# A hybrid decoder layer on one core: the memory loaded transposed with its 1/rms applied at the keys and values, and the final norm in an order written out by hand

## The chip, the cores and the metric

The kernel runs on one core of a Trainium2 chip. The time is device time in microseconds (us) of one execution; the number compared is the median over runs. The engines are TensorE (PE, matrix products; PEld is its loading of weights), VectorE (DVE), ScalarE (ACT), GpSimd (POOL) and SyncE (SP), which here only issues loads. Every engine takes its own instructions in order.

## The reference

One layer on 512 tokens of 1024 channels, with 256 memory tokens, everything in fp32. A mixer with three gated branches, a cross-attention to the memory and a squared-ReLU MLP each add to x; a last norm gives the output. What the change touches:

```python
def rmsnorm(x, g):
    y = x * rsqrt(mean(x * x, axis=-1) + EPS)
    return y * g
...
mem_n = rmsnorm(mem, norm_mem_g)
k, v = split(mem_n @ w_kv, 2)                     # 256 memory tokens, 4 heads x 256
sc = einsum('bshd,bmhd->bhsm', q, k) * 256 ** -0.5
o = einsum('bhsm,bmhd->bshd', softmax(sc), v)
...
x = x + squared_relu_mlp(rmsnorm(x, norm_mlp_g), w_up, w_down)
return rmsnorm(x, final_g)
```

Since 1/rms is one number per token, it commutes with the product: (r * mem * g) @ w = r * ((mem * g) @ w).

## The kernel before

**Products.** Each fp32 operand is split into a high part in the matrix engine's fp32r type and a low part, the rest; a product is three (high x high, high x low, low x high: `mm3`, lines 361 to 363). Weights arrive in chunks of 512 KB on SP's queue (line 304) and are split on the chip: ScalarE casts (line 112), VectorE subtracts (line 113). `split` (lines 350, 351) does this for activations, `split_scaled` (355, 356) with a factor, a number or one value per partition.

**Seven products for eight.** The projections w_o, w_xo and w_down go through `items_w`: a block of 1024 channels is done as seven block products, P1 to P7, of 24 matrix instructions each (line 493). Sums of weights are formed by VectorE (line 131, `plus`) or by a DMA that adds (line 236); results are added to x from the PSUM banks by `add` (lines 128 and 131). For w_o (class `Early`) the order is P1, P2 and P5 in turns, then P6, P3, P7, P4; for w_down (class `Wide`) P1 and P5 in turns, then P6, P3, P2, P7, P4. P7 and P4 finish tokens 256 to 511 (t = 2, 3); P4 goes row by row, so t = 2 is done before t = 3. The hook `after(p)` puts work behind a product.

**Norms.** `norm_begin` sums the squares of half a row block on ScalarE (line 562); `norm_end` does the other half, forms 1/rms (VectorE line 566, GpSimd's power line 556) and multiplies by it and by the gain, which lies broadcast over all partitions (line 584). `norm_T` transposes the result on TensorE (line 593, eight 128 x 128 blocks per 128 tokens, into two PSUM banks of the tag "at") and splits it.

**The memory.** `mem_begin` loads on GpSimd's queue the broadcast gain (512 KB) and the memory's 256 rows (two tiles m_sb of 512 KB). Behind P5 of w_o `mem_norm` norms both tiles; behind P6 and P3 `norm_T` transposes one each into mT (channels on partitions). Then `kv_proj` makes the keys, eight blocks of 24 products with mT moving (256 columns), and the values (mT stationary); `xk_done` and `xv_done` split what comes out. Between the key blocks stand the transposes of the layer's own norm for t = 2, 3. GpSimd's queue is in the written order in this part (`reload_x` enters `manual_schedule` for it).

**The final norm.** Behind P3 of the last block of w_down `norm_begin` sums the finished right halves of t = 0, 1, behind P2 `final` ends them; behind P7 and P4 the same is done for t = 2, 3. `final` is, per t: square sum of the left half, 1/rms, then two products on VectorE (line 1307, left and right 512 columns), each followed by its store, the left on SP's queue, the right on ScalarE's (line 1309).

**Order.** The program is a list of items (`plan`); weights are fetched and split two steps ahead (`pump`, `AHEAD`). The order in which each engine gets its instructions is made before the run by a planner that simulates the kernel with modelled times and goes by the program's order where more than one instruction could go (`schedule_with_timeline_sim`). Inside a `manual_schedule` the named engines keep the program's order. Two of the four "at" banks hold one accumulator from P1 through P6, P7 and P4, two the other from P5 through P3 (`part`, bank names p1 and p3), so that P3's adds free the first two for transposes and P4's adds the others. The large tiles share 30 slots (`unit`), short-lived ones nine (`scr`).

Of the kernel before, what the change touches and what calls it, by code (L numbers as in the profile page):

```python
# [10 lines left out]
F32 = mybir.dt.float32  # L11
F32R = mybir.dt.float32r
AF = mybir.ActivationFunctionType
ALU = mybir.AluOpType
# [24 lines left out]
def trunk_kernel(ctx: ExitStack, tc: tile.TileContext, x, mem, par, rot, dqd, kdec, g_mix, g_xa, g_mem, g_mlp,  # L39
# [50 lines left out]
    gmx = const.tile([P, KT], F32, name="gmx")  # L90

# [381 lines left out]
    def items_w(src, c, pairs, after=lambda p: None, kind=Wide):  # L473
# [4 lines left out]
        def part(p, js, n):  # L478
            bank = dict(P2="p2", P5="p3", P3="p3").get(p, "p1")

            def fn(ws):
# [21 lines left out]
                for i, j in [(i, j) for i in range(2) for j in js] if rows else [(i, j) for j in js for i in range(2)]:  # L503
                    mm(i, j)
                    if j == 1:
                        add(i)
            item(fn, (kind, src, c, n, n + len(js)))
# [45 lines left out]
    def rstd_of(ms, n):  # L553

        r = small.tile([P, n], F32, name="rstd")
        pool.tensor_tensor(out=r, in0=ms, in1=half[:, :n], op=ALU.pow)
        return r
# [516 lines left out]

    def mem_begin():
        S["g_mem"] = load_g(g_mem, pool)
        S["m_sb"] = [unit("m_sb", (P, D), F32) for _ in range(2)]
        for t in range(2):
            pool.dma_start(out=S["m_sb"][t], in_=mem[t * P:(t + 1) * P, :])

    def mem_norm():
        S["mT"] = Split("mT", KT, MEM)
        for t in range(2):
            norm_begin(("m", t), S["m_sb"][t])
            norm_end(("m", t), S["m_sb"][t], S["g_mem"])

    def mem_beside(p):
        if p == "P5":
            item(mem_norm)
        if p in ("P6", "P3"):  # L1090
            t = int(p == "P3")
            item(lambda: norm_T(("m", t), S["mT"], t))
# [24 lines left out]
    def proj_norm(src, name, g, beside, after, first=lambda its: None, kind=Early):  # L1117
# [20 lines left out]
        its = capture(lambda: items_w(src, 0, lambda k: S[name, k // 2].w[k % 2], ends, kind))  # L1138
# [13 lines left out]
    def xk_done(d):  # L1152
        def fn(ps):
            hi, lo = S["kT"](d)
            split(hi, lo, ps[:, :MEM])
        return fn

    def xv_done(c):
        def fn(t, ps):
            hi, lo = S["xv"](t)  # L1160
            cs = slice(c * 512, (c + 1) * 512)
            split(hi[:, cs], lo[:, cs], ps)
        return fn
# [137 lines left out]
    def final(t):  # L1301
        y, ss = S["xn", t], S["ss", t]
        sumsq(S["x"][t], 0, ss, 1, y)
        r = norm_rstd(ss)
        for c, eng in ((0, nc.sync), (1, act)):
            cs = slice(c * 512, (c + 1) * 512)
            dve.scalar_tensor_tensor(out=y[:, cs], in0=S["x"][t][:, cs], scalar=r, in1=S["g"][:, cs],
                                     op0=ALU.mult, op1=ALU.mult)
            eng.dma_start(out=out[t * P:(t + 1) * P, cs], in_=y[:, cs])

    def last(p):
        if p == "P3":
            def begin():
                S["g"] = load_g(g_fin, pool)
                for t in (0, 1):
                    norm_begin(t, S["x"][t], 1)
            item(begin)
        if p == "P2":
            item(lambda: [final(t) for t in (0, 1)])
        if p == "P7":  # L1320
            item(lambda: [norm_begin(t, S["x"][t], 1) for t in (2, 3)])
        if p == "P4":
            item(lambda: [final(t) for t in (2, 3)])

    def down(r):
        items_w(w_down, 8 * r, lambda k: S["u", 2 * r + k // 2].w[k % 2], last if r == NP // 4 - 1 else lambda p: None)
# [66 lines left out]

def _pack_b(w):
# [5 lines left out]
def _lay_out(i):  # L1400
# [10 lines left out]
        "mem": a["mem"][0],  # L1411
# [4 lines left out]
        "g_mix": col(a["norm_mix_g"][0]), "g_xa": a["norm_xa_g"][0], "g_mem": a["norm_mem_g"][0],  # L1416
# [39 lines left out]
```

## Time and profile before

| | us |
|---|---|
| median of 3 runs (1014.11 to 1016.59) | 1015.11 |
| profiled execution, its own time | 1016.54 |
| its span, first to last instruction | 1014.8 |
| TensorE busy | 994.1 |
| VectorE busy | 715.6 |
| ScalarE busy | 526.6 |
| GpSimd busy | 73.4 |

Mean granted TensorE clock: 0.994 of full speed. In the groups a line reads: line of the program, engine, operation, output <- inputs, shape, count, then busy time and mean duration in ns, and behind the bar the idle time ahead of these instructions with what ended it. In a timeline a line begins with start and length in us, and brackets hold a wait and its releaser. Times are from the span's start. A matrix instruction's length includes its way through the pipeline; what it costs in a row of them is the distance between starts.

### The profile page before, as it was taken

Reading aid. Unit: us, or ns where it says so; the run is one execution under the profiler, and the core shown is the slowest. Engines: PE = TensorE matmul, PEld = TensorE weight load, DVE = VectorE, ACT = ScalarE, POOL = GpSimd, SP = SyncE. Lnnn points to the kernel's source line nnn. Section 1 sums busy time; section 2 is a strip of 40 time slices with the busy share of each in tenths; the row PEclk is TensorE's granted clock in tenths of the full one; section 3 lists DMA queues with packets and bytes.
Section 4 is the critical chain, followed back from the end, with each engine's and each line's share of the span. In section 5 each row is a group of like instructions: output and inputs, shape, how many; then the busy total and the mean of one; then the engine's idle time right before and its main releaser. Section 6 shows DMA issues by size and latency. Waiting matters only on the chain.

```text
span 1014.8 us, 13137 instructions
## 1 busy us (share of the span) xinstructions
PE 994.1 (98%) x4958; PEld 841.1 (83%) x4958; DVE 715.6 (71%) x1064; ACT 526.6 (52%) x908; POOL 73.4 (7%) x135
## 2 busy tenths in 40 slices
PE   8999999999999999999989999999999999999996
PEld 6788888878888889988788888879888888888885
DVE  5757787777463787779785466875785785695785
ACT  6556666766433344444654346655544543553543
POOL 1001111223110000001100001110000000000001
PEclk9999999999999999999989999999999999999998
DMA  9332223222122212334555225642044125115212
GB/s 361 129 132 83 83 84 117 80 74 84 63 103 70 77 59 90 122 137 165 169 173 186 84 84 125 165 147 85 20 142 148 43 95 175 63 47 186 80 42 84
DMA packets 32176, 113.08 MB, mean 111 GB/s; under 512 B 3952, under 2 KB 3952, under 8 KB 32112
## 3 DMA queue, kind: packets, MB, share of 16 engines
q1 hardware_dynamic: 28224, 99.65, 28.1%
q0 software_dynamic: 2880, 10.49, 4.4%
q10 hardware_dynamic: 1008, 2.10, 0.6%
q8 instruction: 39, 0.64, 0.2%
q14 instruction: 25, 0.20, 0.1%
HBM read 110.13 MB, written 2.10 MB: 111 GB/s over the span
## 4 chain that ended last, share of the span: by engine, by line
PE 94%; DVE 3%; issue 1%; ACT 1%; POOL 0%; DMA 0%; DVEq 0%; POOLq 0%; SPq 0%
PE mm L362 21%; PE mm L361 21%; PE mm L363 21%; PE p L493 20%; PE p L419 4%; DVE w_part L113 1%; PE o L812 1%; PE aT L778 1%; PE mm L534 1%; PE z L754 0%; PE z L755 0%; DVE x L131 0%; PE at L593 0%; DVE xn L584 0%; PE xsc L363 0%
## 5 line engine op out<-in xcount | busy, mean ns | idle before, releaser
L113 DVE TENSOR_TENSOR w_part<-w_raw,w_part 128x1024 fp32r<-128x1024 f32 (+1 forms) x223 | 269.8, 1212 | 150.6 <-ACT w_part L112 144.1
L112 ACT CAST w_part<-w_raw 128x1024 fp32r<-128x1024 f32 (+1 forms) x223 | 232.3, 1044 | 274.5 <-PE mm L362 130.0
L361 PE MATMUL mm<-hT_h,w_part 128*128 128x512 f32 (+1 forms) x736 | 280.1, 383 | 1.8 <-DVE r_qk L875 1.2
L362 PE MATMUL mm<-hT_l,w_part 128*128 128x512 f32 (+1 forms) x736 | 280.8, 382 | 0.7 <-DVE hT_l L351 0.7
L363 PE MATMUL mm<-hT_h,w_part 128*128 128x512 f32 (+1 forms) x736 | 280.6, 382 | 0.0
L493 PE MATMUL p<-w_part,pr 128*128 128x512 f32 x864 | 201.5, 390 | 0.7 <-DVE w_part L113 0.6
L493 PEld LDWEIGHTS p<-w_part,pr 128*128 128x128 f32 x864 | 161.7, 188 | 35.4 <-DVE x L131 1.0
L361 PEld LDWEIGHTS mm<-hT_h,w_part 128*128 128x128 f32 x736 | 137.8, 188 | 28.0 <-DVE r_qk L875 1.8
L362 PEld LDWEIGHTS mm<-hT_l,w_part 128*128 128x128 f32 x736 | 138.6, 188 | 25.9 <-DVE hT_l L351 1.0
L363 PEld LDWEIGHTS mm<-hT_h,w_part 128*128 128x128 f32 x736 | 138.5, 188 | 25.7
L131 DVE TENSOR_TENSOR w_raw<-w_raw 128x1024 f32<-128x1024 f32 (+1 forms) x46 | 51.7, 1126 | 1.9 <-DMA w_raw<-in_w_o_dram 1.6
L128 DVE TENSOR_TENSOR x<-x,p 128x512 f32<-128x512 f32 x48 | 32.5, 681 | 12.9 <-PE p L493 12.9
L493 PE MATMUL p<-w_part,pr_b 128*128 128x512 f32 x144 | 34.8, 389 | 0.0
L766 DVE TENSOR_TENSOR_SCAN sb_suf<-ones,sb_e 128x128 f32<-128x128 f32 (+3 forms) x32 | 27.4, 856 | 9.5 <-POOL sb_e L745 8.2
L131 DVE TENSOR_TENSOR x<-x,p 128x512 f32<-128x512 f32 x36 | 24.0, 681 | 12.6 <-PE p L493 12.4
L493 PEld LDWEIGHTS p<-w_part,pr_b 128*128 128x128 f32 x144 | 27.0, 188 | 5.6
L769 ACT ACTIVATE sb_suf<-sb_suf 128x128 f32<-128x128 f32 (+3 forms) x32 | 15.1, 472 | 29.6 <-DVE sb_suf L768 29.5
L419 PE MATMUL p<-mix_h,w_part 128*128 128x256 f32 x128 | 25.0, 283 | 0.0
L562 ACT ACTIVATE xn<-x 128x512 f32<-128x512 f32 x24 | 15.1, 630 | 18.0 <-DVE x L128 10.1
L361 PE MATMUL mm<-w_part,xg_h 128*128 128x512 f32 x56 | 21.4, 391 | 0.7 <-DVE sb_v L356 0.7
L362 PE MATMUL mm<-w_part,xg_h 128*128 128x512 f32 x56 | 21.8, 389 | 0.0
L363 PE MATMUL mm<-w_part,xg_l 128*128 128x512 f32 x56 | 21.5, 389 | 0.0
(246 smaller groups left out, 1450.6 us busy)
## 6 DMA issues: line engine op xcount, KB each, us to landing
w_raw<-in_w_in_dram SPq DMA_DIRECT2D x55, 512.0 KB, 3.3
w_raw<-in_w_up_dram SPq DMA_DIRECT2D x32, 512.0 KB, 3.7
w_raw<-in_w_down_dram SPq DMA_DIRECT2D x32, 512.0 KB, 3.4
w_raw<-in_w_br_dram SPq DMA_DIRECT2D x12, 512.0 KB, 3.3
w_raw<-in_w_gate_dram SPq DMA_DIRECT2D x8, 512.0 KB, 3.2
w_raw<-in_w_o_dram SPq DMA_DIRECT2D x8, 512.0 KB, 3.7
w_raw<-in_w_xk_dram SPq DMA_DIRECT2D x8, 512.0 KB, 4.2
w_raw<-in_w_xv_dram SPq DMA_DIRECT2D x8, 512.0 KB, 3.3
```

Source lines behind the costliest of these rows:

```text
L112: act.copy(out=wh, in_=src)
L113: dve.tensor_tensor(out=wl, in0=src, in1=wh.bitcast(F32), op=ALU.subtract)
L128: dve.tensor_tensor(out=out, in0=a, in1=b, op=ALU.subtract)
L131: dve.tensor_tensor(out=out, in0=a, in1=b, op=ALU.add)
L361: te.matmul(ps, lh, rh, start=first, stop=False)
L362: te.matmul(ps, lh, rl, start=False, stop=False)
L363: te.matmul(ps, ll, rh, start=False, stop=last)
L419: te.matmul(ps[:, :256], x[:, k, :], y, start=first and k == 0 and i == 0, stop=k == 3 and i == 2, skip_group_check=True)
L493: te.matmul(acc[bank, i], x, y, start=p in ("P1", "P5", "P2") and j + k + m == 0, stop=j == 1 and k == 1 and m == 2, skip_group_check=True)
L562: act.activation(out=dst[:, cs], in_=src[:, cs], func=AF.Square, accum_out=ss[:, i:i + 1])
L766: dve.tensor_tensor_scan(out=suf[:, :s][:, ::-1], data0=ones[:, :s], data1=e1[:, :s][:, ::-1], initial=0.0, op0=ALU.mult, op1=ALU.add)
L769: act.activation(out=suf[:, :s], in_=suf[:, :s], func=AF.Exp)
```

## The change

The memory is also laid out transposed in the input (1024 channels as 8 x 128 partitions), and loaded so as well: GpSimd's queue now takes the gain as 128 x 8 numbers (gmm), two transposed tiles m_xT of 512 KB and the two m_sb. mT is made without a norm and without TensorE: `mem_part` multiplies four channel blocks by their gain and splits them, behind P5 and behind P6. `mem_rs`, behind P6, sums the squares of m_sb and forms 1/rms for both tiles in one power, and two diagonal matrices; `mem_spread`, behind P3, multiplies ones by them, which puts 1/rms of every memory token on all partitions, and copies it to m_R. `xk_done` multiplies the keys by m_R before their split; `xv_done` uses the split with a factor.

The final norm is cut in three. `final_begin` also multiplies the right half of x by the gain. `final_rstd` ends the square sum and forms 1/rms. `final_out` multiplies the left half by 1/rms and gain on VectorE, as before, and the right half by 1/rms on ScalarE. For the last block's P4 a new hook, `between`, runs when t = 2 is added: it enters a `manual_schedule` of VectorE and ScalarE, so that from there the order is as written: 1/rms of t = 2, the add of t = 3, the output of t = 2, 1/rms of t = 3, its output. For t = 0, 1 both 1/rms now stand ahead of both outputs.

```diff
     def mem_begin():
-        S["g_mem"] = load_g(g_mem, pool)
+        pool.dma_start(out=gmm, in_=g_mem)
+        S["m_xT"] = [unit("m_xT", (P, 4, MEM), F32) for _ in range(2)]
         S["m_sb"] = [unit("m_sb", (P, D), F32) for _ in range(2)]
         for t in range(2):
+            pool.dma_start(out=S["m_xT"][t], in_=mem[MEM + t * P:MEM + (t + 1) * P, :])
+        for t in range(2):
             pool.dma_start(out=S["m_sb"][t], in_=mem[t * P:(t + 1) * P, :])
 
-    def mem_norm():
-        S["mT"] = Split("mT", KT, MEM)
+    def mem_part(j):
+        if j == 0:
+            S["mT"] = Split("mT", KT, MEM)
+        for k in range(4 * j, 4 * j + 4):
+            hi, lo = S["mT"](k)
+            split_scaled(hi, lo, S["m_xT"][j][:, k - 4 * j, :], gmm[:, k:k + 1])
+
+    def mem_rs():
+        ss = small.tile([P, 2], F32, name="ssm")
+        for t, xs in enumerate(S["m_sb"]):
+            act.activation(out=xs, in_=xs, func=AF.Square, accum_out=ss[:, t:t + 1])
+        dve.tensor_scalar(out=ss, in0=ss, scalar1=1.0 / D, scalar2=EPS, op0=ALU.mult, op1=ALU.add)
+        S["m_rs"] = rstd_of(ss, 2, "m_rs")
+        S["m_dg"] = scr("m_dg", (P, 2, P))
         for t in range(2):
-            norm_begin(("m", t), S["m_sb"][t])
-            norm_end(("m", t), S["m_sb"][t], S["g_mem"])
+            dve.tensor_scalar(out=S["m_dg"][:, t, :], in0=ident, scalar1=S["m_rs"][:, t:t + 1], scalar2=None, op0=ALU.mult)
+
+    def mem_spread():
+        r = atps("mrs")
+        te.matmul(r[:, :MEM], ones[:, :P], S["m_dg"].rearrange("p a b -> p (a b)"), start=True, stop=True)
+        S["m_R"] = scr("m_R")
+        act.copy(out=S["m_R"][:, :MEM], in_=r[:, :MEM])
 
     def mem_beside(p):
         if p == "P5":
-            item(mem_norm)
-        if p in ("P6", "P3"):
-            t = int(p == "P3")
-            item(lambda: norm_T(("m", t), S["mT"], t))
+            item(lambda: mem_part(0))
+        if p == "P6":
+            item(lambda: mem_part(1))
+            item(mem_rs)
+        if p == "P3":
+            item(mem_spread)
...
             hi, lo = S["kT"](d)
-            split(hi, lo, ps[:, :MEM])
+            kr = scr("x_k")[:, :MEM]
+            dve.tensor_tensor(out=kr, in0=ps[:, :MEM], in1=S["m_R"][:, :MEM], op=ALU.mult)
+            split(hi, lo, kr)
...
-            split(hi[:, cs], lo[:, cs], ps)
+            split_scaled(hi[:, cs], lo[:, cs], ps, S["m_rs"][:, t:t + 1])
...
-    def final(t):
...
+    def final_rstd(t):
+        ss = S["ss", t]
+        sumsq(S["x"][t], 0, ss, 1, S["xn", t])
+        r = S["r", t] = small.tile([P, 1], F32, name="rf")
+        dve.tensor_scalar(out=r, in0=ss[:, 1:2], scalar1=1.0 / D, scalar2=ss[:, 0:1], op0=ALU.mult, op1=ALU.add)
+        pool.tensor_tensor(out=r, in0=r, in1=half[:, :1], op=ALU.pow)
+
+    def final_out(t):
+
+        y, r = S["xn", t], S["r", t]
+        l, h = slice(0, 512), slice(512, 1024)
+        dve.scalar_tensor_tensor(out=y[:, l], in0=S["x"][t][:, l], scalar=r, in1=S["g"][:, l], op0=ALU.mult, op1=ALU.mult)
+        nc.sync.dma_start(out=out[t * P:(t + 1) * P, l], in_=y[:, l])
+        act.activation(out=y[:, h], in_=y[:, h], func=AF.Copy, scale=r)
+        act.dma_start(out=out[t * P:(t + 1) * P, h], in_=y[:, h])
+
+    def final_begin(t):
+        norm_begin(t, S["x"][t], 1)
+        h = slice(512, 1024)
+        dve.tensor_tensor(out=S["xn", t][:, h], in0=S["x"][t][:, h], in1=S["g"][:, h], op=ALU.mult)
...
         if p == "P2":
-            item(lambda: [final(t) for t in (0, 1)])
+            item(lambda: [f(t) for f in (final_rstd, final_out) for t in (0, 1)])
         if p == "P7":
-            item(lambda: [norm_begin(t, S["x"][t], 1) for t in (2, 3)])
+            item(lambda: [final_begin(t) for t in (2, 3)])
         if p == "P4":
-            item(lambda: [final(t) for t in (2, 3)])
+            item(lambda: (final_out(2), final_rstd(3), final_out(3), S["tail"].__exit__(None, None, None)))
+
+    def between(p):
+
+        if p == "P4":
+            S["tail"] = tc.manual_schedule(engines={dve.engine, act.engine})
+            S["tail"].__enter__()
+            final_rstd(2)
```

More of the change, by code (lines that the diff above doesn't have):

```diff
@@ L90, in trunk_kernel @@
     gmx = const.tile([P, KT], F32, name="gmx")
+    gmm = const.tile([P, KT], F32, name="gmm")
     def load_g(g, eng=None):
@@ L471, in trunk_kernel, with items_w @@
               P7=(2, 1, minus))
-    def items_w(src, c, pairs, after=lambda p: None, kind=Wide):
+    def items_w(src, c, pairs, after=lambda p: None, between=lambda p: None, kind=Wide):
         acc = {}
@@ L506, in fn @@
                         add(i)
+                        if i == 0:
+                            between(p)
             item(fn, (kind, src, c, n, n + len(js)))
@@ L551, in items_m, with rstd_of @@
             item(fn, (kind[min(i, len(kind) - 1)], src, c0 + i))
-    def rstd_of(ms, n):
-        r = small.tile([P, n], F32, name="rstd")
+    def rstd_of(ms, n, name="rstd"):
+        r = small.tile([P, n], F32, name=name)
         pool.tensor_tensor(out=r, in0=ms, in1=half[:, :n], op=ALU.pow)
@@ L1136, in ends @@
             beside(p)
-        its = capture(lambda: items_w(src, 0, lambda k: S[name, k // 2].w[k % 2], ends, kind))
+        its = capture(lambda: items_w(src, 0, lambda k: S[name, k // 2].w[k % 2], ends, kind=kind))
         first(its)
@@ L1298, in trunk_kernel @@
     proj_norm(w_xo, "xo", g_mlp, lambda p: None, first_up, last_heads, Summed)
-    def final(t):
[L1302 to L1309, printed above, removed]
+    def final_rstd(t):
[15 more added lines that the diff above has]
+        dve.tensor_tensor(out=S["xn", t][:, h], in0=S["x"][t][:, h], in1=S["g"][:, h], op=ALU.mult)
     def last(p):
@@ L1315, in begin @@
                 for t in (0, 1):
-                    norm_begin(t, S["x"][t], 1)
+                    final_begin(t)
             item(begin)
         if p == "P2":
-            item(lambda: [final(t) for t in (0, 1)])
+            item(lambda: [f(t) for f in (final_rstd, final_out) for t in (0, 1)])
         if p == "P7":
-            item(lambda: [norm_begin(t, S["x"][t], 1) for t in (2, 3)])
+            item(lambda: [final_begin(t) for t in (2, 3)])
         if p == "P4":
-            item(lambda: [final(t) for t in (2, 3)])
+            item(lambda: (final_out(2), final_rstd(3), final_out(3), S["tail"].__exit__(None, None, None)))
[4 more added lines that the diff above has]
+            final_rstd(2)
     def down(r):
-        items_w(w_down, 8 * r, lambda k: S["u", 2 * r + k // 2].w[k % 2], last if r == NP // 4 - 1 else lambda p: None)
+        items_w(w_down, 8 * r, lambda k: S["u", 2 * r + k // 2].w[k % 2], *((last, between) if r == NP // 4 - 1 else ()))
     for q in range(2, NP):
@@ L1391, in _pack_x, with _pack_mem @@
     return x.T.reshape(4, 2, P, T).transpose(0, 2, 1, 3).reshape(4 * P, 2 * T)
+def _pack_mem(m):
+    return m.T.reshape(2, 4, P, MEM).transpose(0, 2, 1, 3).reshape(2 * P, 4 * MEM)
 def _pack_b(w):
@@ L1410, in _lay_out @@
         "x": np.concatenate([a["x"][0], _pack_x(a["x"][0])], axis=0),
-        "mem": a["mem"][0],
+        "mem": np.concatenate([a["mem"][0], _pack_mem(a["mem"][0])], axis=0),
         "par": par,
@@ L1415, in _lay_out @@
         "kdec": kdec,
-        "g_mix": col(a["norm_mix_g"][0]), "g_xa": a["norm_xa_g"][0], "g_mem": a["norm_mem_g"][0],
+        "g_mix": col(a["norm_mix_g"][0]), "g_xa": a["norm_xa_g"][0], "g_mem": col(a["norm_mem_g"][0]),
         "g_mlp": a["norm_mlp_g"][0], "g_fin": a["final_g"],
```

## The prediction

> **What bounds the kernel now.** I read the page of the profile first: the busy line of the matrix engine and the granted clock over the span.
>
> ```profile
> PE 994.1 (98%) x4958; PEld 841.1 (83%) x4958; DVE 715.6 (71%) x1064; ACT 526.6 (52%) x908; POOL 73.4 (7%) x135
> PEclk9999999999999999999989999999999999999998
> ```
>
> TensorE has 98% of the span, so nothing that shortens another engine's work counts unless TensorE waits for it at that place. There are two places where the clock line isn't 9: slice 21 (from about 507 us) and the last one. They are also the two places that the change touches. So I next asked for the busy times by stretches around the first of them (columns: stretch, length, then busy time and count of each engine, granted clock, DMA).
>
> ```profile
> core 0: us, PE busy (x) PEld busy (x) DVE busy (x) ACT busy (x) POOL busy (x), PEclk, DMA share, GB/s
> 485.00:501.40 16.40, 16.40 (x73) 13.51 (x74) 11.79 (x22) 8.87 (x20) 2.22 (x4) 1.00 0.53 173
> 501.40:508.70 7.30, 6.73 (x34) 5.42 (x33) 7.11 (x8) 6.09 (x10) 0.56 (x2) 1.00 0.48 160
> 508.70:515.40 6.70, 3.83 (x25) 2.80 (x24) 6.70 (x10) 3.74 (x8) 0.00 (x0) 0.88 0.69 234
> 515.40:520.50 5.10, 5.10 (x26) 5.10 (x25) 5.10 (x11) 1.39 (x4) 1.05 (x2) 0.50 0.61 207
> ...
> 523.00:542.40 19.40, 19.40 (x166) 19.40 (x165) 13.91 (x23) 11.47 (x22) 0.00 (x0) 1.00 0.50 164
> ```
>
> From 501.4 to 520.5 VectorE is the one that is full (7.11 of 7.30, 6.70 of 6.70, 5.10 of 5.10) while TensorE has holes; then TensorE runs 5.10 us at half clock. Before and after, TensorE is full and VectorE has room. So this stage, the end of the first residual projection (P7, P4) and the start of the memory's keys, is bound by VectorE, and pays a second time in clock. The timeline of TensorE there, with what ended each wait in brackets:
>
> ```profile
> 501.39 1.03 PE L593 MATMUL at<-ident,xn 128*128 128x128 f32 x8
> 502.18 0.72 PE L493 MATMUL p<-w_part,pr 128*128 128x512 f32 x2
> 503.47 5.29 PE L493 MATMUL p<-w_part,pr 128*128 128x512 f32 x22 [0.57 <-DVE w_part L113]
> 508.60 1.39 PE L593 MATMUL at<-ident,xn 128*128 128x128 f32 x8
> 509.87 0.73 PE L361 MATMUL mm<-mT_h,w_part 128*128 128x256 f32 x4
> 511.18 0.66 PE L593 MATMUL at<-ident,xn 128*128 128x128 f32 x4 [0.58 <-DVE x L131]
> 512.92 0.66 PE L593 MATMUL at<-ident,xn 128*128 128x128 f32 x4 [1.08 <-DVE x L131]
> 514.65 1.11 PE L593 MATMUL at<-ident,xn 128*128 128x128 f32 x4 [1.08 <-DVE mT_l L351]
> 515.42 0.56 PE L362 MATMUL mm<-mT_l,w_part 128*128 128x256 f32 x1
> ...
> 526.51 1.04 PE L593 MATMUL at<-ident,xn 128*128 128x128 f32 x8
> 527.30 0.36 PE L362 MATMUL mm<-mT_l,w_part 128*128 128x256 f32 x1
> ```
>
> The two groups of eight at 501.39 and 508.60 are the memory's transposes; the first product with the memory's low part only starts at 515.42, and every bracket names VectorE.
>
> **Part 1: the transposes go.** At full clock eight transposes occupy TensorE from 526.51 to 527.30, 0.79 us. Sixteen are removed: 1.6 us off TensorE. Their row of work is on the path, since TensorE is never idle for want of other work before 501.4.
>
> **Part 2: VectorE's load before and in the stretch.** Its groups, from 484 to 496 us (first two rows) and from 495.4 to 521 us (the others); behind the bar is the idle time ahead of them:
>
> ```profile
> L113 DVE TENSOR_TENSOR w_part<-w_raw,w_part 128x1024 fp32r<-128x1024 f32 x3 | 3.7, 1224 | 1.0 <-ACT w_part L112 1.0
> L128 DVE TENSOR_TENSOR x<-x,p 128x512 f32<-128x512 f32 x5 | 3.3, 684 | 2.8 <-PE p L493 2.7
> ...
> L351 DVE TENSOR_TENSOR mT_l<-at,mT_h 128x512 fp32r<-128x512 f32 x4 | 2.7, 682 | 0.0
> L584 DVE SCALAR_TENSOR_TENSOR xn<-m_sb,rstd,g_bc 128x1024 f32<-128x1024 f32 x2 | 2.6, 1284 | 0.8 <-POOL rstd L556 0.7
> ```
>
> Removed from the stretch: 2.7 + 2.6 = 5.3 us. What is added has its nearest rows elsewhere in the kernel:
>
> ```profile
> L355 ACT ACTIVATE sb_v<-mm,rstd x8: 463/474/475, 26.6 to 38.8; 128x256 fp32r<-128x256 f32 x8
> L356 DVE SCALAR_TENSOR_TENSOR sb_v<-mm,rstd,sb_v x8: 471/480/488, 28.7 to 42.1; 128x256 fp32r<-128x256 f32 x8
> L655 DVE TENSOR_SCALAR dg<-ident,rstd x4: 492/558/627, 22.9 to 23.8; 128x128 f32<-128x128 f32 x4
> L657 PE MATMUL rsp<-dg,ones x2: 590/590/591, 28.6 to 29.1; 128*128 128x512 f32 x2
> ```
>
> The memory's low parts are eight of the L356 form, 8 x 0.48 = 3.8 us, and the two diagonals 2 x 0.56 = 1.1: 4.9 us. They depend only on loads, and on the memory's own sums, so they can lie at P5 and P6, under the 1.0 + 2.8 us of idle there and the 0.8 us that VectorE waited for the old 1/rms; some 0.3 us remains for the stretch. If that cover were gone, the 4.9 us would undo nearly all of the 5.3. ScalarE gets eight of 0.47 us for four casts and four half squares; it has 8.87 of 16.40 busy there, so I cost it at nothing. The keys get eight more products, by the same 0.48 us 3.8 in all, one for each block of keys; their cover is VectorE's idle time from 523 to 542.4 us, 19.40 - 13.91 = 5.5 us. The values only exchange one form for another of the same shape: nothing.
>
> What TensorE gets back: between 501.39 and 515.42 lie 14.0 us. Its work in them at full clock is 28 transposes (28 x 0.79/8 = 2.8), 24 products of P4 (24 x 0.23 = 5.5, the 0.23 from the run of 48 in Part 4) and four products with the memory (166 rows in 19.40 us above, 0.12 each: 0.5), 8.8 us. So 5.3 us are waits. Both ends are possible: nothing, if VectorE's order leaves the weights' low parts and the residual's adds as late as now, and all 5.3. VectorE is relieved by about as much as TensorE waits, but the brackets show only one wait for the memory itself (1.08); the others are for w_part and for the adds that free the banks, which come earlier only as far as VectorE's queue moves up, and work on xn and hT pushed out of the stretch takes some of the cover of the keys' new products. I take 3.3, the sum of the four bracketed waits.
>
> **Part 3: the clock, the spread and the queues.** At the 0.50 clock 26 rows took 5.10 us, 0.196 each; at 1.00, 166 rows took 19.40, 0.117 each. So the half clock costs 26 x 0.079 = 2.1 us at most, and nothing is won if it stays. I take 1.8: the waits that come before it are the largest from 485 to 542 us. The Trainium skill ("TensorE: Matmul & The Clock Gate", Part 1) says the half clock follows a wholly idle window of about 3.4 us. This trace differs, as no bracket before the fall is above 1.08 us. By that rule the waits would not be the cause and this 1.8 would be 0 (first rival).
>
> The spread of 1/rms is one product of 256 columns; the two rows of L657 start 0.5 us apart for 512 columns and the last takes 0.59, some 1.1 in all, so about 0.6 is added on TensorE. It waits for ScalarE's squares, GpSimd's power and the two diagonals, and TensorE is in order: if that chain comes late, P7 stands behind it, with the old chain as a measure (0.8 us idle on VectorE). I keep 0.5 to 1.5. On the DMA side:
>
> ```profile
> m_sb<-in_mem_dram POOLq DMA_DIRECT2D x2, 512.0 KB, 7.1
> 498.58 0.60 POOL L94 DMA_DIRECT2D g_bc<-in_g_xa_dram  x1
> ```
>
> One 512 KB read more (two transposed halves in, one broadcast gain out) ahead of P1, by the first row at most 7.1 us, on a queue whose data is not used until P5's end: nothing. The second row shows the gain for the queries' norm being asked for only behind the memory's old power on GpSimd; now that load stands ahead of the new power, so it comes earlier, and the power waits behind its issue, 0.60 us, inside the spread's 0.5 to 1.5.
>
> Sum of the middle: 1.6 + 3.3 + 1.8 - 0.6 = 6.1 us gained.
>
> **Part 4: the end.** Timeline rows of the tail, and the landing time of the output's transfers:
>
> ```profile
> 994.08 1.22 DVE L113 TENSOR_TENSOR w_part<-w_raw,w_part 128x1024 fp32r<-128x1024 f32 x1 [0.77 <-ACT w_part L112]
> 995.74 11.07 PE L493 MATMUL p<-w_part,pr 128*128 128x512 f32 x48
> 1006.48 1.41 DVE L1307 SCALAR_TENSOR_TENSOR xn<-x,rstd,g_bc 128x512 f32<-128x512 f32 x2 [0.72 <-POOL rstd L556]
> 1007.81 0.68 DVE L131 TENSOR_TENSOR x<-x,p 128x512 f32<-128x512 f32 x1
> 1008.52 0.63 ACT L562 ACTIVATE xn<-x 128x512 f32<-128x512 f32 x1 [2.95 <-DVE x L131]
> 1010.15 1.41 DVE L1307 SCALAR_TENSOR_TENSOR xn<-x,rstd,g_bc 128x512 f32<-128x512 f32 x2 [0.72 <-POOL rstd L556]
> 1011.60 0.34 ACTq L1309 DMA_DIRECT2D out_dram<-xn  x1
> DMA to landing us min/median/max: 2.0/2.1/2.2
> ```
>
> TensorE's last product ends at 995.74 + 11.07 = 1006.81, but the last add starts at 1007.81, because the finished tokens of t = 2 stand ahead of it on VectorE. With the order written by hand the add is first: about 1.0 us sooner. Its chain (square, power) is unchanged. At the end two products follow each other on VectorE (1.41) before the last transfer is issued; now one of 0.7 runs beside one on ScalarE, for which the nearest row is the 0.63 of a square of the same size: 0.7 us sooner. Sum 1.7. The low end is 0.6: ScalarE now does t = 2's right columns and issues their transfer (0.34) ahead of t = 3's square, and its half may end last. The four new products of x with the gain, 0.68 each by L128, lie where VectorE waits for TensorE (the adds of P2, P7, P4); without that cover they would delay P4's weights by 1.4 us, whose last part is done at 994.08 + 1.22 = 995.3 and used halfway through the run of 48, at 1001.3: 6 us of lead.
>
> **The sum.** 6.1 + 1.7 = 7.8 us. The profiled execution took 1016.54 us (span 1014.8, 1.7 around it), so it becomes 1008.7; that run lies 1.4 above the median of 1015.11, so a median of 1007.3.
>
> **The rivals.** The forecast, TensorE getting back most of its waits and clock, has 0.56.
>
> *The half clock stays*, 0.20. The keys' first blocks still start after a ragged stretch (the residual's transposes wait for banks as now), and some 26 rows run at 0.196 again. For it: the clock fell after waits of a microsecond, and these need not all go. Then 7.8 - 1.8 = 6.0: 1009.1. The Trainium skill's rule on the clock gate, cited above, leads here too, for another reason.
>
> *VectorE gives it back*, 0.17. The order of VectorE's and ScalarE's queues is made by a planner before the run; if it leaves P4's weights behind P7's adds and the memory's parts in the stretch, waits and clock stay, and the change doesn't do what it is built to do in the middle. Then 1.6 - 0.6 + 1.7 = 2.7: 1012.4, inside the 0.3% (3 us) that a measurement of this kernel can't tell from none.
>
> *VectorE holds the keys*, 0.07, the one on the other side. Each block of keys is 24 products, 24 x 0.117 = 2.8 us. VectorE's share of a block is a weight part 1.22, the new product 0.48, and low parts of keys and of two transposed pieces of h, some 3 x 0.45: 3.1 us. If the planner packs h's pieces in as tightly as that, TensorE waits in each block, and the half clock spreads. Price: 24 x 0.079 = 1.9 us a block; four more blocks make 7.6, less the 2.7: 4.9 slower, 1020.0. It decides from the point where two pieces of h meet each block; against it speaks the 5.5 us of idle VectorE shows over seven blocks now.
>
> **How the numbers follow.** Faster by over 0.3% are the first two cases, 0.76; the third is within, 0.17; the last slower, 0.07. The low end has all waits and clock and the cheapest spread: 1.6 + 5.3 + 2.1 - 0.5 + 1.7 = 10.2, thus 1004.9, less 1 for the scatter of three runs: 1003.9. The high end is the third case with 0.6 of scatter, 1013.0; the last case is left out. The forecast's own range is 1004 to 1010.
>
> **What would show it.** Right: no transposes from the memory, the first product with the memory's low part within 1 us behind P4's last, P4 ending near 507, the clock at 1.0 in all stretches from 500 to 530, 192 products of keys at 0.12; in the tail the last add within 0.1 us of TensorE's end and the last two transfers issued about 3.1 us after it. Wrong: brackets on TensorE that name w_part or x as long as now, a wait ahead of the spread's product, or a clock of 0.50 in the keys. The forecast falls if VectorE is still full from 501 to 520 us.

## The result and the profile after

The kernel after takes 1008.81 us (median of 4 runs, 1008.41 to 1009.54), the kernel before beside it 1015.25 (4 runs, 1014.11 to 1016.59): ratio 0.9941, 95% interval 0.9929 to 0.9953. That is 6.4 us between the medians, and 7.9 between the profiled executions (1016.54 and 1008.65, spans 1014.8 and 1006.9). Ratios, here and below, are the measurement's own estimates and not quotients of two medians (0.9937 here). Two executions below were disturbed (1671.03 us, the profiled one of early_g, and 2582.99 us, one of the kernel before beside it) and are left out, so early_g has three runs and no trace.

The page of after, its busy line and granted clock:

```profile
PE 989.5 (98%) x4944; PEld 836.9 (83%) x4944; DVE 716.9 (71%) x1073; ACT 531.2 (53%) x913; POOL 73.7 (7%) x136
PEclk9999999999999999999999999999999999999998
```

Slice 21 is back at 9. The same stretches as in the prediction, of after (stretch, length, busy time and count of each engine, granted clock, DMA):

```profile
501.40:508.70 7.30, 6.59 (x28) 4.80 (x28) 7.04 (x10) 5.77 (x9) 0.53 (x2) 1.00 0.45 142
508.70:515.40 6.70, 6.70 (x57) 6.62 (x56) 6.70 (x10) 3.98 (x9) 0.43 (x1) 1.00 0.84 287
515.40:520.50 5.10, 5.10 (x45) 5.10 (x45) 5.10 (x10) 3.08 (x7) 0.66 (x2) 1.00 0.71 247
...
523.00:542.40 19.40, 19.40 (x137) 18.19 (x136) 15.83 (x31) 10.99 (x20) 0.00 (x0) 1.00 0.56 179
```

TensorE is full from 508.7 on and the clock stays at 1.00. But VectorE is as full as before (7.04, 6.70, 5.10): the engine that the prediction called the bound wasn't relieved, and TensorE runs all the same. TensorE's timeline of after, from w_o's first product to the first product of the values:

```profile
468.24 1.98 PE L494 MATMUL p<-w_part,pr 128*128 128x512 f32 x8
...
502.22 0.49 PE L494 MATMUL p<-w_part,pr 128*128 128x512 f32 x1 [0.22 <-DVE x L129]
502.61 0.70 PE L1107 MATMUL mrs<-m_dg,ones 128*128 128x256 f32 x2
503.74 3.02 PE L494 MATMUL p<-w_part,pr 128*128 128x512 f32 x12 [0.43 <-DVE w_part L114]
...
509.36 1.03 PE L596 MATMUL at<-ident,xn 128*128 128x128 f32 x8
...
535.36 0.40 PE L362 MATMUL mm<-w_part,mT_h 128*128 128x512 f32 x1
```

The first row is cut off by its window, which ends at 470. The only waits left are P4's: 0.22 for an add and 0.43 for its weight part. P4 ends at 509.3 (its last ten products run from 506.83 to 509.29), later than before (503.47 + 5.29 = 508.76) and not near 507; everything is won behind it, where the keys and the transposes of the layer's own norm ("own transposes" from here on) stand without a bracket.

That was not won by a VectorE that makes its adds sooner. Two of the waits of before, 0.58 and 1.08, ended with VectorE's adds of P4's sums, which free banks. Those two adds in before and in after:

```profile
510.45 0.68 DVE L131 TENSOR_TENSOR x<-x,p 128x512 f32<-128x512 f32 x1
512.18 0.68 DVE L131 TENSOR_TENSOR x<-x,p 128x512 f32<-128x512 f32 x1
```

```profile
510.88 0.68 DVE L132 TENSOR_TENSOR x<-x,p 128x512 f32<-128x512 f32 x1
512.61 0.68 DVE L132 TENSOR_TENSOR x<-x,p 128x512 f32<-128x512 f32 x1
```

They come 0.43 us later in after, and no instruction of TensorE stands waiting for them any more. The third wait of before, 1.08, ended when VectorE had read some of the memory's transposes out of their bank; in after there are none. What does come sooner is the memory's low parts: the last is done at 498.5, against 516.3 before.

The two ends of the middle in before, w_o's first product and the values' first:

```profile
468.39 1.98 PE L493 MATMUL p<-w_part,pr 128*128 128x512 f32 x8
...
542.51 0.40 PE L361 MATMUL mm<-w_part,mT_h 128*128 128x512 f32 x1
```

So the middle went from 74.1 us (542.51 - 468.39) to 67.1 (535.36 - 468.24): 7.0 gained. I use this distance for every kernel below. The tail of after:

```profile
988.56 11.04 PE L494 MATMUL p<-w_part,pr 128*128 128x512 f32 x48
...
999.64 0.69 DVE L132 TENSOR_TENSOR x<-x,p 128x512 f32<-128x512 f32 x1 [1.03 <-PE p L494]
...
1000.40 0.63 ACT L565 ACTIVATE xn<-x 128x512 f32<-128x512 f32 x1 [0.41 <-DVE x L132]
...
1002.78 0.37 ACTq L1343 DMA_DIRECT2D out_dram<-xn  x1
```

TensorE ends at 999.60 (988.56 + 11.04) and the span at 1006.9: 7.3 us, against 8.0 before (1014.8 - 1006.81). The tail gave 0.7 of the 1.7 forecast.

All runs in one table (us; "middle" is w_o's first product to the values' first, "tail" TensorE's end to the span's end, both of the profiled execution; ratio to the kernel before on the same chip, with its interval):

| kernel | median | ratio | middle | tail |
|---|---|---|---|---|
| before | 1015.25 | | 74.1 | 8.0 |
| after | 1008.81 | 0.9941 (0.9929 to 0.9953) | 67.1 | 7.3 |
| mem_alone | 1009.49 | 0.9947 (0.9932 to 0.9962) | 67.1 | 8.1 |
| tail_alone | 1013.94 | 0.9991 (0.9982 to 1.0000) | 72.9 | 7.2 |
| tail_vec | 1010.36, one run | | 67.2 | 8.6 |
| early_rs | 1014.38 | 0.9995 (0.9985 to 1.0004) | 73.0 | 7.3 |
| dve_load | 1010.27 | 0.9950 (0.9935 to 0.9966) | 68.3 | 7.3 |
| pe_T | 1009.23 | 0.9939 (0.9923 to 0.9954) | 67.6 | 7.3 |
| no_spread | 1008.76 | 0.9934 (0.9916 to 0.9952) | 66.9 | 7.3 |
| early_g | 1010.68 | 0.9953 (0.9936 to 0.9971) | | |
| old_early | 1017.26 | 1.0024 (1.0015 to 1.0033) | 75.6 | 8.0 |
| tail_q | 1008.69 | 0.9935 (0.9922 to 0.9949) | 67.2 | 7.1 |
| banks | 1011.49 | 0.9960 (0.9946 to 0.9974) | 70.4 | 8.0 |
| banks_late | 1008.99 | 0.9948 (0.9932 to 0.9965) | 66.7 | 8.0 |

### The profile page after: what moved, and what is told of

Read it like the earlier page. It is cut to its first block, busy times and chain, and to the rows that moved or that the text cites. A ratio compares the mean times of both kernels' runs of the same rounds, so it can differ in the third digit from the quotient of the medians.

```text
span 1006.9 us, 13109 instructions
## 1 busy us (share of the span) xinstructions
PE 989.5 (98%) x4944; PEld 836.9 (83%) x4944; DVE 716.9 (71%) x1073; ACT 531.2 (53%) x913; POOL 73.7 (7%) x136
## 4 chain that ended last, share of the span: by engine, by line
PE 92%; DVE 3%; DMA 2%; issue 1%; ACT 1%; POOL 0%; SPq 0%; POOLq 0%; DVEq 0%
PE mm L362 21%; PE mm L363 21%; PE mm L364 21%; PE p L494 20%; PE p L420 4%; DVE w_part L114 1%; PE o L815 1%; DMA x<-in_x_dram 1%; PE aT L781 1%; DMA w_raw<-in_w_in_dram 1%; PE z L757 0%; PE z L758 0%; PE at L596 0%; PE xsc L363 0%; PE xsc L364 0%
```

## The experiments

The theory of the prediction is *load*: TensorE waited because VectorE had 5.3 us of the memory's work in the stretch. The rival that the profile after suggests is *order*: TensorE waited because products and transposes stood in its queue ahead of the time at which their operands and banks came, whatever VectorE's total; with the memory's parts early, the planner lays TensorE's queue out otherwise. The expectations name the two in words of their own; from old_early on the second is called "need" and then "order alone".

**Each half of the change alone.** mem_alone keeps the old tail, tail_alone the old memory:

```diff
-            item(lambda: (final_out(2), final_rstd(3), final_out(3), S["tail"].__exit__(None, None, None)))
+            item(lambda: [final(t) for t in (2, 3)])
...
```

> The memory's part alone, the final norm as before. From the trace of the changed kernel (values of the memory start 7.1 us sooner, TensorE's last product 7.2 us sooner, but the end only 0.7 more) the theory is that the middle brings 7.0 us and the tail 0.7: this kernel is then 7 us below the kernel before by profile (span near 1007.7). The rival is the split of the prediction, 6.1 and 1.7: span near 1008.7.

```diff
-            item(lambda: mem_part(0))
...
+            item(mem_norm)
...
```

> The final norm's part alone, the memory as before. Theory: TensorE's end to the span's end shrinks from 8.0 us to about 7.3, so 0.7 us or 0.07%, within noise of the median; the half clock at the keys is there as before. Rival (the prediction's term): 1.7 us, a TensorE end to span's end of 6.3.

Both theories came, and the two halves add up: 0.53% and 0.09% against 0.59%, middle 7.0 and tail 0.8 (the interval of tail_alone alone reaches no change). tail_alone's middle of 72.9 is not the tail's doing; its half clock lasted half as long as in the profile of before (last section).

**What in the tail.** tail_vec gives the right columns back to VectorE and keeps the written order:

```diff
-        act.activation(out=y[:, h], in_=y[:, h], func=AF.Copy, scale=r)
+        dve.tensor_scalar(out=y[:, h], in0=y[:, h], scalar1=r, scalar2=None, op0=ALU.mult)
```

> The changed kernel, but the right columns of the output are multiplied by 1/rms on VectorE behind the left ones, in the same written order. Theory: the last two stores, 512 KB together, run one after the other on the same DMA engines (before, 0.67 us each at 390 GB/s), so issuing the second 0.7 us sooner gains nothing: from TensorE's last product to the span's end it takes 7.3 us, as in the changed kernel, within 0.3, although the last issue is 0.7 us later. Rival: the end follows the last issue at a fixed distance, and it takes 8.0.

Neither number came, for a reason of the order itself. The tail of tail_vec (TensorE's end 1000.13):

```profile
1001.95 0.34 ACTq L1343 DMA_DIRECT2D out_dram<-xn  x1
1002.33 0.63 ACT L565 ACTIVATE xn<-x 128x512 f32<-128x512 f32 x1 [3.44 <-DVE xn L1342]
...
1004.74 0.33 SPq L1341 DMA_DIRECT2D out_dram<-xn  x1
1005.14 0.34 ACTq L1343 DMA_DIRECT2D out_dram<-xn  x1
```

ScalarE's issue of t = 2's store, which now waits for VectorE, stands ahead of t = 3's square, so the square starts 2.2 us behind TensorE's end instead of 0.80. But from that square to the span's end the three kernels agree: 6.3 us before (1008.52 to 1014.8), 6.5 after (1000.40 to 1006.9), 6.4 here (1002.33 to 1008.7), although the last issue comes 3.1, 2.4 and 2.8 us behind the square. What they share is the first of the last two issues, 2.4 us behind the square in each (here 1004.74, in after 1002.78). In before it is this row, and the bytes then move in this stretch (the last columns are the DMA engines' busy share and GB/s):

```profile
1010.93 0.33 SPq L1309 DMA_DIRECT2D out_dram<-xn  x1
1011.60 0.34 ACTq L1309 DMA_DIRECT2D out_dram<-xn  x1
```

```profile
1010.00:1011.60 1.60, 0.00 (x0) 0.00 (x0) 1.41 (x2) 0.00 (x0) 0.12 (x1) 0.50 0.00 0
1011.60:1013.20 1.60, 0.00 (x0) 0.00 (x0) 0.00 (x0) 0.00 (x0) 0.00 (x0) 0.50 0.87 326
```

The same of after:

```profile
1003.50:1005.10 1.60, 0.00 (x0) 0.00 (x0) 0.00 (x0) 0.00 (x0) 0.00 (x0) 0.50 0.87 328
```

Some 0.8 us behind the first issue (at 1011.7 in before, 1003.6 in after) the DMA engines fill up and move both stores' 512 KB in one burst of 1.4 to 1.5 us. The second store, issued 0.7 us later in before, still rides in it: the first store's half of the bytes takes that long. So ScalarE's half of the output, which brought the second issue forward, bought nothing; the 0.7 of the tail is the order: the last add first, its square 0.80 us behind TensorE's end (1000.40 - 999.60) instead of 1.71 (1008.52 - 1006.81).

tail_q halves the pieces of the last output, to start the burst sooner:

```diff
+        n = 256 if t == 3 else 512
+        for c in range(0, 512, n):
+            l, h = slice(c, c + n), slice(512 + c, 512 + c + n)
...
```

> The changed kernel, with the last tokens' four half rows written in quarters: VectorE and ScalarE each finish 256 columns, hand them to their store, and then the next 256. If the transfer of the last 512 KB (1.45 us in both kernels) is what follows the last issue, the bytes start some 0.35 us sooner and the stretch from TensorE's end to the span's end falls from 7.3 to 6.9 or 7.0 us, the time by 0.3 to 0.4 us. If what follows the last issue is a fixed time for each store, then the last issue, now some 0.1 to 0.4 us later (two products and two issues in place of one), sets the end: 7.4 to 7.7 us, 0.1 to 0.4 us slower.

```profile
1001.01 0.63 ACT L565 ACTIVATE xn<-x 128x512 f32<-128x512 f32 x1 [0.42 <-DVE x L132]
...
1003.17 0.37 ACTq L1345 DMA_DIRECT2D out_dram<-xn  x1
...
1004.13 0.34 ACTq L1345 DMA_DIRECT2D out_dram<-xn  x1
```

The tail was 7.1. The first issue comes 2.16 us behind the square, 0.2 sooner than in after, and the tail is 0.2 shorter, though the last issue (1004.13) comes 0.7 later: here too the end goes with the first issue. It came 0.2 sooner and not 0.35, because half the columns took more than half the time. The tail lies between the two forecasts, and the medians of tail_q and after can't be told apart.

**VectorE's load and the transposes, given back.** dve_load adds 5.3 us of work that nobody uses to VectorE, behind P6 and P3; pe_T adds sixteen transposes that nobody uses at the old places. Each calls its own `extra` from the same two places:

```diff
+            item(lambda: extra(0))
...
+            item(lambda: extra(1))
```

> The changed kernel with the VectorE work that the change removed put back as work that nobody needs: two products of 128x1024 behind P6 and two subtractions of 128x512 behind P6 and behind P3, 5.3 us by the rows of before (2.6 + 2.7); no transposes come back. Theory A, VectorE's load made the waits and through them the half clock: 3 to 6 us above the changed kernel (1012 to 1015), the keys' first blocks at 0.5 clock again. Theory B, what cost was that the keys needed the transposed parts, and that the transposes of the layer's own norm stood ahead of the keys in TensorE's order: within 1 us of the changed kernel, the clock stays at 1.0.

> The changed kernel with sixteen transposes of the memory on TensorE put back behind P6 and P3, into two banks each of the tag at, read by ScalarE in one column only; nobody needs them, and VectorE gets no work. By the prediction's term they cost their own 1.6 us (16 x 0.1): 1010.4. Theory B's part on the banks: they hold the two free banks, so that the transposes of the layer's own norm come later, and the cost is 1 to 3 us more than the 1.6, with a wait on TensorE in front of one of the two groups.

dve_load lost 1.5 us (1.2 in the middle), outside both forecasts but far from the 5.3 that it put back. It lost them in one place, and no half clock came:

```profile
505.21 3.01 PE L494 MATMUL p<-w_part,pr 128*128 128x512 f32 x12 [1.63 <-DVE w_part L114]
```

P4's weight part, queued behind the useless work, waits 1.2 us longer than in after (0.43). The keys run through, although VectorE is busy 19.40 of the 19.40 us from 523 to 542.4. pe_T lost 0.4 us (0.5 in the middle), less than either forecast:

```profile
501.33 1.03 PE L1116 MATMUL at<-ident,m_sb 128*128 128x128 f32 x8
...
503.26 0.60 PE L1116 MATMUL at<-ident,m_sb 128*128 128x128 f32 x4
503.80 3.03 PE L494 MATMUL p<-w_part,pr 128*128 128x512 f32 x12
506.67 0.60 PE L1116 MATMUL at<-ident,m_sb 128*128 128x128 f32 x4
```

Twelve of the sixteen lie where TensorE would wait for P4's weight part: without them the x12 started at 503.74, with them at 503.80. Transposes at that place are nearly free; the last four, at 506.67, stand where nothing is waited for. So neither the load nor the transposes, each given back alone, carry the 7.0; the two together weren't given back to this kernel.

**The spread.** no_spread leaves out the 1/rms of the memory at the keys: diagonals, product, copy and the eight products of VectorE.

```diff
...
-            kr = scr("x_k")[:, :MEM]
-            dve.tensor_tensor(out=kr, in0=ps[:, :MEM], in1=S["m_R"][:, :MEM], op=ALU.mult)
-            split(hi, lo, kr)
+            split(hi, lo, ps[:, :MEM])
```

> The changed kernel without 1/rms at the keys: no diagonals, no spread, no product with it; the keys' rows are left unscaled (the values' are scaled). From the trace of the changed kernel TensorE loses 502.61 to 503.74 around the spread, so 0.7 to 1.1 us less than the changed kernel, if the keys' eight products on VectorE are covered; if they are not (the prediction's rival on the other side) 2 us or more less.

Its middle is 66.9, 0.2 less than after's, and its median 0.05 less, where 0.7 to 1.1 were forecast: the spread too lies in P4's wait, and the keys' eight products under VectorE's room.

**The spread sooner.** early_rs puts the memory's sums behind P5 and the spread behind P6; early_g also loads the queries' gain with the memory:

```diff
-        r = atps("mrs")
+        r = mmps("mrs")
...
         if p == "P5":
+            item(mem_rs)
             item(lambda: mem_part(0))
         if p == "P6":
+            item(mem_spread)
             item(lambda: mem_part(1))
-            item(mem_rs)
-        if p == "P3":
-            item(mem_spread)
```

> The changed kernel with the memory's square sums and 1/rms behind P5 and the spread behind P6, its product in a bank of the tag mm (P2's are free then) instead of behind P3 in a bank of the tag at. Theory: the 1.7 us that TensorE loses between P7 and P4 (from 501.5 to 503.74, less 0.5 of the spread's own work) come from the squares of the memory and the two diagonals standing ahead of P4's weight parts on ScalarE and VectorE; moved ahead, they fall under idle time, and the kernel is 1.0 to 1.7 us below the changed kernel (about 1007.4). Rival: P4's weight parts wait on VectorE for P7's last add whatever stands beside it, and it is within 0.5 us of the changed kernel.

> The slow variant (sums behind P5, spread behind P6) with one edit: the gain of the layer's own norm is loaded on GpSimd's queue with the memory, ahead of the memory's power, instead of behind it (in the slow variant at 500.70, in the changed kernel at 482.16). Theory G, that variant is slow because the load of the gain stood behind the memory's power: TensorE's wait of 3.3 us for xn goes, and it is within 1 us of the changed kernel. Theory P, what decides is the planner's order of TensorE, which still puts eight transposes of the layer's norm between two halves of P4, and VectorE's, which now puts both xn (2.5 us) ahead of P4's first weight part: it stays 2 us or more above the changed kernel.

Meant to free P4, early_rs lost 5.6 us, which neither theory had. Of early_rs, TensorE, and GpSimd's queue:

```profile
506.40 1.68 PE L596 MATMUL at<-ident,xn 128*128 128x128 f32 x8 [3.27 <-DVE xn L587]
508.73 5.26 PE L494 MATMUL p<-w_part,pr 128*128 128x512 f32 x12 [0.64 <-DVE w_part L114]
```

```profile
500.70 0.60 POOL L95 DMA_DIRECT2D g_bc<-in_g_xa_dram  x1
```

The planner put eight own transposes inside P4. Their gain was asked for only at 500.70, behind the memory's power on GpSimd's queue (482.16 in after), and landed 4.0 us later, at 504.7. By the trace the 1/rms of their own tokens came last, at 505.03: its sums stood behind four of the memory's low parts on VectorE (502.57 to 504.15). TensorE stood 3.27 us for them and then ran P4 at half clock. With the gain early (early_g) 3.7 of the 5.6 come back; whether by the load itself or by the order that the planner then made isn't shown, as early_g has no trace. It stays 1.9 above after, between its two forecasts (1 and 2). Early_rs speaks for *order*: VectorE's load is after's.

**The old work in another order.** This decides. old_early puts the old memory norm behind P2 and its transposes behind P5 and P6, in banks of the other kind:

```diff
-        if p == "P5":
+        if p == "P2":
             item(mem_norm)
-        if p in ("P6", "P3"):
+        if p in ("P5", "P6"):
...
-            item(lambda: norm_T(("m", t), S["mT"], t))
+            item(lambda: norm_T(("m", t), S["mT"], t, mmps))
```

> The kernel before, with its old memory norm, its sixteen transposes and its old tail, but the memory's norm is put behind P2 instead of P5 and its transposes take banks of the mm kind instead of the at kind, so that all sixteen stand ahead of P4 and the own transposes no longer stand ahead of the keys' products. All of VectorE's and TensorE's old work is still done. Theory 'need': the 7.0 us of the middle came from the memory's low parts being ready and from free banks when the keys begin, not from less work on VectorE; then the first values product comes within 2 us of the changed kernel's 535.2 us (535.5 to 537.2), no half clock, the span 1008.0 to 1009.7, the time 1009.8 to 1011.5, ratio 0.995 to 0.9965. Theory 'load': the 5.3 us of VectorE's work and the 1.6 us of transposes had to go; then TensorE waits as before for x and w_part, the first values product comes at 541 to 543 us and the time is 1014 to 1016.5. In between (538 to 541) each would have a part.

It was slower than before, outside both forecasts, and is no test yet: the waits at the start of the keys were gone, but a load of w_o and the gain had slipped behind the memory's power on GpSimd's queue (499.15 and 499.76), and TensorE stood later, whether for that reason isn't shown:

```profile
525.58 0.63 PE L593 MATMUL at<-ident,xn 128*128 128x128 f32 x4 [2.82 <-DVE hT_l L351]
528.84 2.80 PE L593 MATMUL at<-ident,xn 128*128 128x128 f32 x12 [2.64 <-DVE hT_l L351]
```

banks leaves all items where they were in before and changes only the banks, so that the queue of loads stays:

```diff
-            item(lambda: norm_T(("m", t), S["mT"], t))
+            item(lambda: norm_T(("m", t), S["mT"], t, mmps))
```

> The kernel before with one word changed: the memory's sixteen transposes take banks of the mm kind instead of the at kind, whose four are held by the sums p1 and p3 until P3's and P4's adds. All of VectorE's and TensorE's old work stays, the loads and GpSimd's queue keep their order (in old_early the last w_o load and the queries' gain had slipped behind the memory's power). The planner now puts all sixteen ahead of P4 and only eight own transposes between P4 and the keys. Theory 'need': the memory's low parts are ready when the keys begin, so TensorE runs through the keys at full clock: first values product at 535.5 to 538 us, against 542.4 before and 535.2 in the changed kernel; the time 1009.8 to 1012. Theory 'load': VectorE, with the same 5.3 us of memory work, is late with something else by as much: a wait of 2 us or more for hT_l, w_part or mT_l somewhere from 503 to 530, half clock behind it, first values product at 540 us or later, the time 1013 to 1016.5. If the waits only move and shrink (each under 1 us, no half clock) the truth is between, 538 to 540.

```profile
501.54 1.91 PE L593 MATMUL mm<-ident,xn 128*128 128x128 f32 x16
503.20 5.73 PE L493 MATMUL p<-w_part,pr 128*128 128x512 f32 x24
508.76 1.03 PE L593 MATMUL at<-ident,xn 128*128 128x128 f32 x8
...
524.54 1.07 PE L593 MATMUL at<-ident,xn 128*128 128x128 f32 x8 [1.92 <-DVE hT_l L351]
...
538.88 0.40 PE L361 MATMUL mm<-w_part,mT_h 128*128 128x512 f32 x1
```

Of the 7.0, 3.8 come from the banks: all sixteen transposes stand ahead of P4, and P4 and the keys' first blocks run through, sooner than in after (508.76 against 509.36). A new wait of 1.92 for own transposes and one stretch of half clock behind it (525.8 to 529.1) took the rest. The time is that of *order*, the first values product (538.9) lies between the two theories' numbers. VectorE, full from 508.7 to 527 us, had not freed the banks of hT in time, as *load* has it. But the transposes there need not be asked for so soon, and banks_late moves them back:

```diff
             if p == "P7":
...
-                item(lambda: norm_T(0, S["hT"], 0))
+                if name != "mp":
+                    item(lambda: norm_T(0, S["hT"], 0))
...
-            if d in (2, 4):
-                last_T(2 + d // 4)
+            for t in range(NT):
+                if d == (1, 3, 5, 6)[t]:
+                    last_T(t)
```

> The kernel of the run banks (the old memory norm and transposes, in mm banks), and the thirty-two transposes of the queries' own norm entered in the program behind the keys' blocks 1, 3, 5 and 6 instead of behind P7, P4 and blocks 2 and 4; the planner then has eight of them ahead of the keys as in banks, eight in the third block, and the other sixteen from the sixth block on. No work is taken from any engine. Theory 'order alone': the 1.92 us that TensorE waited for hT_l in banks, and the 1.5 us of half clock behind it, came from own transposes asked for sooner than VectorE could free their banks; placed later they cost nothing, and the first values product comes 67 to 68 us behind the first product of w_o (before 74.1, banks 70.4, the changed kernel 67.1): the time 1009.2 to 1010.3 without the new tail, so the memory's new layout would not have been needed for its gain. Theory 'load': VectorE is full to 529 us and the 5.3 us turn up elsewhere, as a wait of over 1.5 us for w_part, xk_l or hT_l later in the keys or at the queries: 69.5 us or more to the values or as much lost behind them, the time 1011 to 1013.

```profile
501.40:508.70 7.30, 7.30 (x44) 6.23 (x42) 7.26 (x8) 6.82 (x12) 0.41 (x1) 1.00 0.45 154
508.70:515.40 6.70, 6.70 (x59) 6.70 (x58) 6.70 (x11) 4.07 (x9) 0.00 (x0) 1.00 0.54 172
515.40:520.50 5.10, 5.10 (x45) 5.10 (x45) 5.10 (x10) 2.93 (x6) 1.93 (x2) 1.00 0.94 306
```

```profile
468.24 1.98 PE L493 MATMUL p<-w_part,pr 128*128 128x512 f32 x8
...
534.97 0.40 PE L361 MATMUL mm<-w_part,mT_h 128*128 128x512 f32 x1
```

It takes 1008.99 us with the old memory norm, the old sixteen transposes and the old tail; the middle is 66.7, 0.4 less than after's. The gain for the queries is asked for at 498.43, as late as in before (498.58), so its earlier load in after (482.16) isn't the cause either. VectorE is full in these rows as in before, TensorE has no hole, the clock is 1.00. All 48 transposes, 16 of the memory and 32 own, still lie ahead of the values' first product. What VectorE does in the 19.1 us differs: nine weight parts for the coming products instead of seven (10.7 us against 8.4, and 10.8 in after), and less of the own norm, which is put off. So the middle's whole gain can be had without taking any work away: the order was the cause. With the new tail besides, 0.7 less would be expected, some 1008.3; that was not run.

## Why the prediction was right and where it was wrong

The case that was forecast came: faster, within the range, 1.5 us above the number. Several steps were wrong, and some of the errors cancel.

- **"This stage ... is bound by VectorE"** is the step that failed. The busy share said so, the brackets named VectorE, and VectorE is just as busy in after and in banks_late. A bracket names who released an instruction, not that the releaser had no time: what was late was the place in the queues. So the sign given for its fall ("if VectorE is still full from 501 to 520 us") came true while the time came in.
- **"Removed from the stretch: ... 5.3 us"** was misread too. The two norm products of the memory (2.6) stand at 496.56 and 498.65 in before, ahead of the stretch in which VectorE is full; only the 2.7 of the low parts lie in it, half of what TensorE waited.
- **Transposes, 1.6.** Sixteen of them given back to after cost 0.5 in the middle (pe_T), and with all sixteen the middle of banks_late lies below after's. "TensorE is never idle for want of other work before 501.4" is true and was the wrong question: just behind 501.4 TensorE waits for P4's weights.
- **Waits, 3.3 of 5.3.** All three waits behind P4 went, 2.7 together. P4's own stayed, since its weight part still stands behind P7's last add on VectorE (and now the two diagonals, 502.08 to 502.56); hence P4's end at 509.3 and not 507.
- **Half clock, 1.8 of 2.1 "at most".** All of it went, and it was more. The 26 rows counted begin at 515.4, but the clock fell at 513.9; TensorE was busy 2.65 and 3.40 us at half clock (next section), and half of that, 3.0, is an estimate of what it cost.
- **Spread, 0.6.** It cost 0.2, in the shade of P4's wait. Together the middle was 7.0 where 6.1 were forecast: waits and clock make 5.7 of it, and how the other 1.3 divide isn't settled by a run.
- **Tail, 1.7.** The add came first, 0.04 us behind TensorE's end, as forecast, and the square 0.9 sooner; 0.2 of that were lost again behind the square. The other 0.7, for ScalarE's half, was nothing: the sum ended at the last issue, though the first one sets when the bytes of both leave.
- **From the profile to the median.** Profile to profile 7.8 were forecast and 7.9 came, 1008.7 against 1008.65. That closeness is luck: the middle was 0.9 too low and the tail 1.0 too high. The median was then set 1.4 lower because the profiled run of before lay 1.4 above its median. This failed: that run most likely lay high by a stretch of half clock which the change removes (next section; argued, not traced), and the runs of after lie within 1.1 us. It is nearly the whole error of 1.5.
- **The rivals.** "VectorE gives it back" came true in its condition for P4's weights, not in its price. "VectorE holds the keys" didn't come: VectorE has 15.83 of 19.40 us in the keys and TensorE has no hole. In "the half clock stays", the Trainium skill ("TensorE: Matmul & The Clock Gate", Part 1) was read as saying that the waits weren't the cause, since no wait filled its window of about 3.4 us. The runs agree with the length of the window and not with its being wholly idle, as the next rows show.

## What the runs showed of the clock

The half clock came in stretches of 3.4 us. Of before and of tail_alone, windows laid to the change of the clock:

```profile
510.50:513.90 3.40, 1.42 (x9) 0.84 (x8) 3.40 (x5) 2.47 (x7) 0.00 (x0) 0.99 0.76 247
513.90:517.30 3.40, 2.65 (x13) 2.65 (x14) 3.40 (x9) 0.88 (x3) 0.76 (x2) 0.50 0.82 277
517.30:520.70 3.40, 3.40 (x18) 3.40 (x18) 3.29 (x5) 0.51 (x2) 0.29 (x1) 0.50 0.47 160
```

```profile
510.80:514.20 3.40, 1.31 (x8) 0.84 (x8) 3.40 (x5) 1.99 (x6) 0.00 (x0) 1.00 0.80 243
514.20:517.60 3.40, 3.13 (x15) 3.13 (x16) 3.40 (x8) 1.36 (x4) 1.06 (x2) 0.50 0.82 281
517.60:521.00 3.40, 3.40 (x31) 3.40 (x31) 3.28 (x7) 0.74 (x4) 0.00 (x0) 0.99 0.36 130
```

The fall follows a window in which TensorE was busy 1.42 and 1.31 of 3.40 us, by waits of 1.1 at most. One window at half clock follows, and a second where the first wasn't nearly full (2.65 against 3.13). banks fell after 1.48 of 3.40 and had one window. But dve_load was busy only 1.77 in one window (502.5 to 505.9) and 1.28 in another (502.0 to 505.4) and fell in none, and old_early, whose clock fell at 528.0, did not fall at 524.7 although TensorE was busy only some 1.5 of the 3.4 us ahead of that. That the windows lie on a grid of their own, as the Trainium skill ("TensorE: Matmul & The Clock Gate", Part 1) says when it calls the window free-running, would explain dve_load; the runs here don't settle it, nor how idle a window must be.

The half clock may also explain the scatter of before. Its runs beside the experiments lie in three groups by mean clock: 1013.5 to 1014.5 us at 0.998, 1014.1 to 1015.6 at 0.996 and 0.997, 1016.0 to 1017.4 at 0.994 and 0.995. The profiled run (1016.54, 0.994) has two windows, tail_alone's (0.997) one. The mean alone doesn't count windows, since the idle end of a run lies at half clock too (from 1001.6 of 1006.9 us in after, whose mean is 0.997 without a window in the middle). That the median of before has one is argued from these, not traced.

## What to carry to other kernels

When an engine's brackets name a busy engine, ask first whether the waiting instruction had to stand there: moving transposes to other banks and later places cost two small edits and won what a new memory layout won. Look whether the releaser came any sooner in the faster kernel: here VectorE's adds came later. Read what a wait already hides before pricing work that is taken away from beside it, and look at what a moved step does to the queue of loads, which changed in two experiments here that lost time. A profiled run that lies off its median may lie off for a reason; if the change removes the reason, the offset isn't to be subtracted again.
